# The load of the joint exp-and-ln tables held behind the last eight silus instead of the one traced last

## The chip, the core and the metric

The kernel runs on one core of a Trainium2 chip. The metric is the device time of one execution in microseconds (us), as the median of the runs. Beside the runs there is one profiled execution, whose trace gives the start and the length of each instruction on each engine. PE is the matmul engine, DVE the vector engine, ACT the engine that evaluates functions such as exp, ln and silu from tables, POOL the general-purpose engine, SP the engine that issues most of the DMAs. Every engine works through its own instructions strictly in their order.

## The reference, cut to what matters

The kernel computes a trunk of two layers on an input of 512 tokens by 1024 columns. Layer 0 mixes tokens by attention, layer 1 by a gated delta rule; each mixer stands between two half-step SwiGLU feed-forward networks (FFNs). All is float32, and the matmuls are made of three passes over split operands to keep that precision. The change concerns the first FFN, which uses silu, and the attention that follows it, which uses exp and ln:

```
def swiglu(h, w_gate, w_up, w_down):
    return (jax.nn.silu(h @ w_gate) * (h @ w_up)) @ w_down

# stick-breaking attention, block of 128 queries (4 heads of 128)
z = jnp.einsum('bqhd,bkhd->bhqk', qb, k) * scale
log_beta = jax.nn.log_sigmoid(z)
log_keep = jnp.where(earlier, jax.nn.log_sigmoid(-z), 0.0)
log_after = lax.cumsum(log_keep, axis=3, reverse=True) - log_keep
a = jnp.where(earlier, jnp.exp(log_beta + log_after), 0.0)
return jnp.einsum('bhqk,bkhd->bqhd', a, v)
```

The other four heads use differential attention, which is a softmax (exp, no ln) with a subtraction.

## The kernel before

Activations are kept transposed, as eight tiles of 128 columns by 512 tokens. Weights come in panels of 512 KB by DMA (tile `raw`), which ACT rounds into `wh` (line 173) and DVE turns into the remainder `wl` (line 174); three buffers of each are in rotation. `mm3` (lines 180 to 182) then makes three matmuls of each pair. The matmuls collect in tiles called `mm` (two buffers), `pa` and `pb` (three each).

The first FFN ends in the function `seven`, whose silus are at line 534: four of them, of 128x256, for each pair of hidden tiles. Behind it `even_mixer` opens the attention and calls `exp_ln_tables`, which adds an instruction to ACT's stream that loads the table set holding both exp and ln. [...] A scheduler decides where each instruction stands in its engine's stream, by dependences; the load has no data, so it is tied by hand to an activation that it must stand behind. Once the streams are fixed, the build goes through ACT's stream and adds a load of its own in front of each activation whose function is not in the set then held.

The attention runs in four groups of two heads, two of differential attention (`diff_block`), then two of stick-breaking attention (`sb_block`). While the blocks of one group are worked, the projections of the next group, or the output projection, run between them on PE. In each of the two stick-breaking groups eight blocks (two heads by four query blocks of 128x128 to 128x512) go through this chain, up to three at a time:

```
        nc.vector.tensor_tensor(z[:, :n], ps[:, :n], strict[:, (3 - i) * P:], op=ALU.add)
        nc.scalar.activation(e[:, :n], z[:, :n], AF.Abs)
        nc.scalar.activation(e[:, :n], e[:, :n], AF.Exp, scale=-1.0)
        nc.scalar.activation(e[:, :n], e[:, :n], AF.Ln, bias=1.0)
        nc.vector.scalar_tensor_tensor(s[:, :n], z[:, :n], 0.0, e[:, :n], ALU.max, ALU.add)
        nc.vector.tensor_tensor_scan(r[:, :n][:, ::-1], self.ones.broadcast_to([P, n]),
        nc.vector.tensor_tensor(r[:, :n], z[:, :n], r[:, :n], op=ALU.subtract)
        nc.scalar.activation(r[:, :n], r[:, :n], AF.Exp)
        aT = self.trans_block(pool, r, i)
```

In the profile these are lines 811 (z), 813 (abs), 815 (exp), 816 (ln), 819 (s), 822 (scan), 825 (subtraction) and 826 (the second exp). `trans_block` turns r by PE transposes (line 799) and copies them from `pa` (line 801, on ACT); line 832 multiplies with the values, and line 834 copies the result out. Line 663 scales the projected queries out of an `mm` tile on DVE, line 374 adds the output projection to x on DVE, and line 790 copies a finished differential head out of `pa` on ACT.

Of the kernel before, what the change touches and what calls it, by code (L numbers as in the profile page):

```python
# [12 lines left out]
AF = mybir.ActivationFunctionType  # L13
# [74 lines left out]
class Ordered:  # L88


    def __init__(self, tc):
        self.tc, self.engine = tc, tc.nc.tensor
# [8 lines left out]
class Trunk:  # L101
# [4 lines left out]
    def __init__(self, ctx, tc):  # L106
        self.tc = tc
        self.nc = tc.nc
        self.const = ctx.enter_context(tc.tile_pool(name="const", bufs=1))
        self.xp = ctx.enter_context(tc.tile_pool(name="xp", bufs=1))  # L110
        self.wp = ctx.enter_context(tc.tile_pool(name="wp", bufs=4))
        self.np_ = ctx.enter_context(tc.tile_pool(name="np", bufs=2))
        self.ps = ctx.enter_context(tc.tile_pool(name="ps", bufs=2, space=bass.MemoryType.PSUM))
        self.dram = ctx.enter_context(tc.tile_pool(name="dr", bufs=1, space=bass.MemoryType.DRAM))
        self.ahead, self.pending, self.pin = [], [], None
        self.te = self.nc.tensor
        self.x = [self.xp.tile([P, T], F32, name=f"x{c}") for c in range(KC)]
        self.consts()
# [65 lines left out]
    def exp_ln_tables(self):  # L184

        nc = self.nc
        ld = nc.scalar.add_instruction(mybir.InstLoadActFuncSet(
            name=nc.get_next_instruction_name(), act_func_set_id=EXP_LN_SET, ins=[], outs=[]))
        dep = mybir.DependencyInfo(mybir.DependencyClass.NoSync, mybir.DependencyReason.DATA)
        self.tc.add_manual_dep(ld.ins, self.last_act.ins.name, dep, reason="tables")  # L190
        return ld, dep


# [222 lines left out]
    def eight(self, pool, wg, wu, f, first):  # L416

        nc = self.nc
        g = self.proj_pair(wg, f * P, (self.a_ps, self.b_ps) if f == 2 else None,
                           2 if first and f == 0 else 1)  # L420
        u = self.proj_pair(wu, f * P, (self.a_ps, self.b_ps))
        for j in range(2):
            gr, sg, ur, hd = (self.small(pool, t) for t in ("gr", "sg", "ur", "hd"))
            nc.vector.tensor_tensor(gr, g[j], self.rb, op=ALU.mult)
            self.last_act = nc.scalar.activation(sg, gr, AF.Silu)
            nc.vector.tensor_tensor(ur, u[j], self.rb, op=ALU.mult)
            nc.vector.tensor_tensor(hd, sg, ur, op=ALU.mult)  # L427
            yield hd
# [35 lines left out]
    def seven(self, pool, wg, wu, f):  # L464

        nc = self.nc
        x8 = lambda t: t.rearrange("p (x c) -> p x c", x=8)
        def load(eng, v, kh, lo, hi, **kw):  # L470
            for q, w in enumerate((wg, wu)):
                eng.dma_start(v[:, q * 4:q * 4 + 4], w[kh * 512:(kh + 1) * 512,  # L472
                                                       f * P + lo:f * P + hi]
                              .rearrange("(k p) c -> p k c", p=P), **kw)
        raw = lambda: x8(self.wp.tile([P, 1024], F32, tag="raw", name="raw", bufs=NRAW))
        add = dict(accum_op=ALU.add)
        b11 = x8(pool.tile([P, 1024], F32, tag="sb", name="sb"))
        load(nc.sync, b11, 0, 0, P)
        b2 = x8(pool.tile([P, 2048], F32, tag="sr", name="sr"))
        load(nc.sync, b2, 1, 0, 2 * P)  # L480
        t1, t3 = x8(pool.tile([P, 1024], F32, tag="t1", name="t1")), raw()
        load(nc.sync, t1, 0, 0, P)
        load(nc.gpsimd, t1, 0, P, 2 * P, **add)
        load(nc.sync, t3, 0, P, 2 * P)
        load(nc.gpsimd, t3, 1, P, 2 * P, **add)
        b21, b22 = b2[:, :, :P], b2[:, :, P:]
        X, Y, Z = self.mm_ps(), self.a_ps(), self.b_ps()

        def product(ps, o, right, start=False):
            h = x8(self.wp.tile([P, 1024], F32R, tag="wh", name="wh", bufs=NSPL))  # L490
            l = x8(self.wp.tile([P, 1024], F32R, tag="wl", name="wl", bufs=NSPL))
            self.split_to(h, l, right)
            ah, al = self.left[o]
            for q in range(2):
                out = ps[:, q * 256:(q + 1) * 256]
                for k in range(4):
                    a = [t[k // 2][:, k % 2] for t in (ah, al)]
                    for i, (wt, xt) in enumerate(((h, a[0]), (h, a[1]), (l, a[0]))):
                        nc.tensor.matmul(out, lhsT=wt[:, q * 4 + k], rhs=xt,  # L499
                                         start=start and q + k + i == 0,  # L500
                                         stop=q == 1 and k == 3 and i == 2, skip_group_check=True)

        def combine(tag, a, b, op):
            t = self.small(pool, tag)
            nc.vector.tensor_tensor(t, a, b, op=op)
            return t

        product(X, 0, b11, True)
        p1 = self.np_.tile([P, T], F32, tag="acc", name="p1", bufs=1)
        nc.scalar.copy(out=p1, in_=X)  # L510
        t2 = raw()
        with self.tc.issue_after(self.met) if self.met else nullcontext():
            nc.vector.tensor_tensor(t2, t1, b22, op=ALU.add)
        product(Y, 1, t2, True)
        u2 = self.np_.tile([P, T], F32, tag="sq", name="u2")
        nc.vector.tensor_tensor(u2, p1, Y, op=ALU.add)
        product(Z, 2, t1, True)
        product(Y, 3, t3)
        u3 = self.np_.tile([P, T], F32, tag="sq", name="u3")
        nc.vector.tensor_tensor(u3, p1, Y, op=ALU.add)  # L520
        c22 = self.small(pool, "gr")
        self.met = nc.vector.tensor_tensor(c22, Z, u3, op=ALU.subtract).ins
        product(X, 4, b21)
        t4 = raw()
        nc.vector.tensor_tensor(t4, t2, b21, op=ALU.add)
        product(Y, 5, t4)
        c21 = combine("ur", p1, Y, ALU.add)
        product(Z, 6, b22)
        c12 = combine("ur", Z, u2, ALU.subtract)
        for lo, hi in ((X, c21), (c12, c22)):  # L530
            sg, hd = self.small(pool, "sg"), self.small(pool, "hd")
            for i, c in enumerate((lo, hi)):
                s = slice(i * 256, (i + 1) * 256)
                self.last_act = nc.scalar.activation(sg[:, s], c[:, :256], AF.Silu)
                nc.vector.tensor_tensor(hd[:, s], sg[:, s], c[:, 256:], op=ALU.mult)
            yield hd

# [791 lines left out]
```

## Time and profile before

| | us |
|---|---|
| median of 3 runs | 2018.27 |
| lowest and highest run | 2018.04 and 2020.41 |
| the profiled execution, its own time | 2018.62 |
| its span, first to last instruction | 2016.9 |
| PE busy in the span | 1967.6 (98%) |
| DVE busy | 1304.0 (65%) |
| ACT busy | 897.3 (44%) |

The span begins with the first instruction; 1.7 us of the profiled execution's time lie outside it. Busy shares are means over stages with different limits: one stage can wait for an engine that is idle half of the time in the whole.

### The profile page before, as it was taken

How to read it: one execution, taken by the hardware profiler on the slowest of the kernel's cores; microseconds unless marked ns; L12 is line 12 of the kernel's file. 1: busy time of each engine (PE TensorE's matmuls, PEld its weight loads, DVE VectorE, ACT ScalarE, POOL GpSimd, SP SyncE). 2: the span in 40 equal slices, each digit the busy share in tenths (PEclk: the TensorE clock that was granted, in tenths of full speed). 3: DMA queues.
4: the chain of work that ended last, by engine and by line, in shares of the span. 5: the costliest groups of instructions: out<-in, count | busy, mean ns of one | idle time of the engine just before them, and what ended most of it. 6: DMA issues, size and time to landing. Idle time of an engine off the chain costs nothing.

```text
span 2016.9 us, 29447 instructions
## 1 busy us (share of the span) xinstructions
PE 1967.6 (98%) x11514; PEld 1720.1 (85%) x11514; DVE 1304.0 (65%) x2058; ACT 897.3 (44%) x1577; POOL 254.6 (13%) x394
## 2 busy tenths in 40 slices
PE   8999999999899999999999999998899999999998
PEld 7899898888778899998889999876787788888887
DVE  6867485796557776575677667577577575443543
ACT  5434254466874344353334434455455453222322
POOL 1021110100000021110103011005441400000000
PEclk9999999999999999999999999999999999999999
DMA  7568453221135487543648654344333233322331
GB/s 200 151 132 209 92 128 105 88 83 53 47 88 136 127 171 176 114 105 106 156 131 173 167 125 95 106 116 107 80 81 86 72 110 94 95 94 94 97 101 73
DMA packets 291263, 230.28 MB, mean 114 GB/s; under 512 B 31618, under 2 KB 266420, under 8 KB 291124
## 3 DMA queue, kind: packets, MB, share of 16 engines
q1 hardware_dynamic: 209604, 195.21, 31.7%
q0 software_dynamic: 50688, 25.17, 10.2%
q10 hardware_dynamic: 30832, 8.02, 1.7%
q8 instruction: 90, 1.47, 0.3%
q14 instruction: 49, 0.40, 0.1%
HBM read 223.10 MB, written 5.26 MB: 113 GB/s over the span
## 4 chain that ended last, share of the span: by engine, by line
PE 60%; POOL 5%; DMA 2%; DVE 2%; issue 1%; ACT 1%; ACTq 0%; POOLq 0%; DVEq 0%
PE pa L499 7%; PE pa L182 5%; PE pa L180 5%; PE pa L181 5%; PE pb L182 5%; PE pb L180 5%; PE pb L181 5%; PE mm L95 5%; PE pb L499 5%; PE mm L499 5%; PE mm L181 3%; PE mm L182 3%; PE mm L180 3%; POOL tmp L1162 2%; POOL rr L1165 2%
## 5 line engine op out<-in xcount | busy, mean ns | idle before, releaser
L174 DVE TENSOR_TENSOR wl<-raw,wh 128x1024 fp32r<-128x1024 f32 (+1 forms) x252 | 295.4, 1173 | 271.6 <-ACT wh L173 270.7
L173 ACT CAST wh<-raw 128x1024 fp32r<-128x1024 f32 (+1 forms) x252 | 254.4, 1010 | 427.8 <-PE pb L181 153.5
L180 PE MATMUL mm<-xnh,wh 128*128 128x512 f32 (+1 forms) x432 | 168.7, 394 | 7.9 <-DVE qT L663 5.6
L182 PE MATMUL mm<-xnh,wl 128*128 128x512 f32 (+1 forms) x432 | 168.6, 392 | 0.0
L181 PE MATMUL mm<-xnl,wh 128*128 128x512 f32 (+1 forms) x432 | 168.2, 390 | 0.0
L226 DVE TENSOR_TENSOR wl<-raw,wh 128x1024 fp32r<-128x1024 f32 x72 | 88.0, 1223 | 79.0 <-ACT wh L225 79.0
L225 ACT CAST wh<-raw 128x1024 fp32r<-128x1024 f32 x72 | 75.5, 1049 | 113.6 <-PE pb L499 43.9
L95 PE MATMUL mm<-xnh,wh 128*128 128x512 f32 x256 | 109.1, 426 | 12.9 <-DVE cx L1051 12.9
L499 PE MATMUL pa<-sx,wh 128*128 128x256 f32 x576 | 109.9, 283 | 0.0
L180 PEld LDWEIGHTS mm<-xnh,wh 128*128 128x128 f32 x432 | 82.9, 192 | 25.5 <-DVE qT L663 6.6
L181 PE MATMUL pa<-hid,wh 128*128 128x512 f32 x264 | 102.8, 389 | 0.0
L182 PE MATMUL pa<-hid,wl 128*128 128x512 f32 x264 | 102.7, 389 | 0.0
L181 PE MATMUL pb<-hid,wh 128*128 128x512 f32 x264 | 102.7, 389 | 0.0
L182 PE MATMUL pb<-hid,wl 128*128 128x512 f32 x264 | 102.7, 389 | 0.0
L180 PE MATMUL pa<-hid,wh 128*128 128x512 f32 x264 | 102.3, 389 | 0.0
L180 PE MATMUL pb<-hid,wh 128*128 128x512 f32 x264 | 102.2, 389 | 0.0
L472 POOL DMA_DIRECT2D raw<-in_ffn_w_gate_dram x24 | 30.9, 1289 | 561.0 <-DMA raw<-in_ffn_w_gate_dram 306.8
L95 PE MATMUL mm<-xnl,wh 128*128 128x512 f32 x256 | 101.6, 397 | 0.0
L95 PE MATMUL mm<-xnh,wl 128*128 128x512 f32 x256 | 101.5, 396 | 0.0
L182 PEld LDWEIGHTS mm<-xnh,wl 128*128 128x128 f32 x432 | 82.7, 191 | 15.9 <-issue 0.5
L181 PEld LDWEIGHTS mm<-xnl,wh 128*128 128x128 f32 x432 | 82.8, 192 | 15.6 <-issue 0.2
L225 ACT CAST hid<-hd 128x512 fp32r<-128x512 f32 x88 | 54.5, 619 | 81.3 <-DVE hd L427 72.9
(395 smaller groups left out, 5626.8 us busy)
## 6 DMA issues: line engine op xcount, KB each, us to landing
raw<-in_ffn_w_down_dram SPq DMA_DIRECT2D x88, 512.0 KB, 3.7
raw<-in_ffn_w_gate_dram SPq DMA_DIRECT2D x40, 512.0 KB, 3.7
raw<-in_ffn_w_up_dram SPq DMA_DIRECT2D x40, 512.0 KB, 3.6
raw<-in_gdn_w_in_dram SPq DMA_DIRECT2D x32, 512.0 KB, 3.9
sr<-in_ffn_w_gate_dram SPq DMA_DIRECT2D x24, 512.0 KB, 3.8
sr<-in_ffn_w_up_dram SPq DMA_DIRECT2D x24, 512.0 KB, 4.9
raw<-in_att_w_in_dram SPq DMA_DIRECT2D x24, 512.0 KB, 3.6
sb<-in_ffn_w_gate_dram SPq DMA_DIRECT2D x24, 256.0 KB, 3.8
```

Source lines behind the costliest of these rows:

```text
L95: return self.tc.keep_in_program_order(self.engine.matmul(*args, **kw))
L173: nc.scalar.copy(out=h[:, :n], in_=raw[:, :n])
L174: nc.vector.tensor_tensor(l[:, :n], raw[:, :n], h[:, :n].bitcast(F32), op=ALU.subtract)
L180: self.te.matmul(out, lhsT=lh, rhs=rh, start=start, stop=False)
L181: self.te.matmul(out, lhsT=lh, rhs=rl, start=False, stop=False)
L182: self.te.matmul(out, lhsT=ll, rhs=rh, start=False, stop=stop)
L225: nc.scalar.copy(out=h, in_=src)
L226: nc.vector.tensor_tensor(l, src, h.bitcast(F32), op=ALU.subtract)
L472: eng.dma_start(v[:, q * 4:q * 4 + 4], w[kh * 512:(kh + 1) * 512, f * P + lo:f * P + hi] .rearrange("(k p) c -> p k c", p=P), **kw)
L499: nc.tensor.matmul(out, lhsT=wt[:, q * 4 + k], rhs=xt, start=start and q + k + i == 0, stop=q == 1 and k == 3 and i == 2, skip_group_check ...
L1162: nc.gpsimd.tensor_tensor(p, rr[:, :k, j:j + 1].broadcast_to(sh), lb[:, j, j + 1:].rearrange("p (o m) -> p o m", o=1) .broadcast_to(sh), o ...
L1165: nc.gpsimd.tensor_tensor(rr[:, :k, j + 1:], rr[:, :k, j + 1:], p, op=ALU.subtract)
```

## The change

The silus are gathered in a list, and the hand-made tie of the load is made to each of the last eight instead of to the one that was traced last. The eight are those of the last two pairs of hidden tiles.

```
-        self.ahead, self.pending, self.pin = [], [], None
+        self.ahead, self.pending, self.pin, self.silus = [], [], None, []
...
-        self.tc.add_manual_dep(ld.ins, self.last_act.ins.name, dep, reason="tables")
+        for act in self.silus[-8:]:
+            self.tc.add_manual_dep(ld.ins, act.ins.name, dep, reason="tables")
...
-            self.last_act = nc.scalar.activation(sg, gr, AF.Silu)
+            self.silus.append(nc.scalar.activation(sg, gr, AF.Silu))
...
-                self.last_act = nc.scalar.activation(sg[:, s], c[:, :256], AF.Silu)
+                self.silus.append(nc.scalar.activation(sg[:, s], c[:, :256], AF.Silu))
```

One line more in the function moves the numbers of all later lines up by one in the changed kernel: the silu at line 534 is at line 535 there, the ln of line 816 at line 817.

ACT's stream at the end of the first FFN, before the change. `sg` is the output of a silu, `ur` its input, `hid` a finished hidden tile; the load at line 187 is the one that `exp_ln_tables` adds, and that at line 534 one that the build added.

```order
L534 ACTIVATE sg<-gr 128x256
L187 ACT_TABLE_LOAD
L173 CAST wh<-raw 128x1024
L534 ACT_TABLE_LOAD
L534 ACTIVATE sg<-ur 128x256
L173 CAST wh<-raw 128x1024
L225 CAST hid_3276<-hd 128x512
L534 ACTIVATE sg<-ur 128x256
L225 CAST hid_3285<-hd 128x512
```

The same place in the changed kernel:

```order
L535 ACTIVATE sg<-gr 128x256
L173 CAST wh<-raw 128x1024
L535 ACTIVATE sg<-ur 128x256
L173 CAST wh<-raw 128x1024
L226 CAST hid_3276<-hd 128x512
L535 ACTIVATE sg<-ur 128x256
L187 ACT_TABLE_LOAD
L226 CAST hid_3285<-hd 128x512
```

The load of line 187 has moved behind the last two silus, and the load at line 534, which brought silu's set back, is gone.

ACT's stream in the first stick-breaking group, before the change; `e` and `r` are the tiles of the chain above.

```order
L801 COPY aT<-pa 128x128
L816 ACT_TABLE_LOAD
L816 ACTIVATE e<-e 128x384
L826 ACT_TABLE_LOAD
L826 ACTIVATE r<-r 128x256
L816 ACT_TABLE_LOAD
L816 ACTIVATE e<-e 128x384
L813 ACTIVATE e<-z 128x512
L815 ACT_TABLE_LOAD
L815 ACTIVATE e<-e 128x512
L816 ACT_TABLE_LOAD
L816 ACTIVATE e<-e 128x512
```

The same place in the changed kernel:

```order
L802 COPY aT<-pa 128x128
L817 ACTIVATE e<-e 128x384
L827 ACTIVATE r<-r 128x256
L817 ACTIVATE e<-e 128x384
L814 ACTIVATE e<-z 128x512
L816 ACTIVATE e<-e 128x512
L817 ACTIVATE e<-e 128x512
```

The activations stand in the same order, and every load between them is gone. Over the whole program ACT has 30 loads fewer: 28 in the two stick-breaking groups (16 and 12), the one at line 534, and one at line 626, the first exp of the attention. The streams of PE, DVE, POOL and SP are the same in both kernels, row by row.

## Rows read from the trace of the kernel before

**Rows 1.** Busy us by stretch: window, length, PE, PEld, DVE, ACT, POOL, clock, DMA, GB/s

```profile
312.00:330.00 18.00, 18.00 (x113) 16.22 (x112) 10.74 (x15) 9.47 (x13) 0.00 (x0) 1.00 0.41 133
384.00:394.00 10.00, 10.00 (x75) 9.53 (x75) 9.77 (x18) 9.62 (x14) 0.00 (x0) 1.00 0.18 54
486.00:524.00 38.00, 29.07 (x140) 22.48 (x139) 18.23 (x44) 35.39 (x58) 2.06 (x2) 0.91 0.09 28
548.00:584.00 36.00, 31.51 (x139) 24.34 (x137) 21.97 (x41) 34.78 (x60) 0.00 (x0) 0.91 0.12 37
```

**Rows 2.** PE's waits from 484 to 602: total, times, longest

```profile
PE mm L180 <- DVE qT L663: 5.6, 1, 5.6
PE pa L832 <- ACT aT L801: 4.1, 3, 2.0
PE pa L799 <- ACT r L826: 2.0, 1, 2.0
PE mm L180 <- DVE x L374: 1.4, 1, 1.4
PE pa L799 <- ACT mf L790: 1.0, 1, 1.0
```

**Rows 3.** ACT's groups by line: count, busy us, mean ns, idle before

```profile
L816 ACT ACT_TABLE_LOAD x14 | 18.0, 1283 | 0.2
L826 ACT ACT_TABLE_LOAD x9 | 11.5, 1283 | 0.2
L815 ACT ACT_TABLE_LOAD x5 | 6.4, 1283 | 0.1
...
L816 ACT ACTIVATE e<-e 128x128 f32<-128x128 f32 (+3 forms) x16 | 7.3, 468 | 0.2
...
L534 ACT ACT_TABLE_LOAD x1 | 1.3, 1283 | 0.0
```

**Rows 4.** ACT in order of time, stick-breaking groups: start, length

```profile
490.73 1.28 ACT L816 ACT_TABLE_LOAD   x1
...
513.06 1.28 ACT L816 ACT_TABLE_LOAD   x1
514.36 0.52 ACT L816 ACTIVATE e<-e 128x384 f32<-128x384 f32 x1
...
551.45 1.28 ACT L816 ACT_TABLE_LOAD   x1
...
577.68 1.28 ACT L816 ACT_TABLE_LOAD   x1
```

**Rows 5.** DVE in order of time: start, length, in brackets the wait before

```profile
514.91 0.56 DVE L819 SCALAR_TENSOR_TENSOR s<-z,e 128x384 f32<-128x384 f32 x1 [3.01 <-ACT e L816]
515.39 0.68 DVE L663 SCALAR_TENSOR_TENSOR qT<-mm,rb 128x512 f32<-128x512 f32 x1
```

**Rows 6.** Busy time around PE's low clock, columns as in rows 1

```profile
512.00:516.00 4.00, 0.00 (x0) 0.00 (x0) 1.09 (x2) 3.94 (x6) 0.00 (x0) 0.63 0.00 0
516.00:520.00 4.00, 3.88 (x9) 3.08 (x10) 0.75 (x3) 3.96 (x8) 0.00 (x0) 0.52 0.00 0
568.00:574.00 6.00, 5.18 (x15) 4.37 (x16) 5.30 (x9) 5.91 (x10) 0.00 (x0) 0.50 0.11 32
```

**Rows 7.** PE in order of time, first and last of runs of 128x512 matmuls

```profile
516.12 0.79 PE L180 MATMUL mm<-xnh,wh 128*128 128x512 f32 x1 [5.63 <-DVE qT L663]
...
520.01 0.40 PE L180 MATMUL mm<-xnh,wh 128*128 128x512 f32 x1
...
556.14 0.39 PE L182 MATMUL mm<-xnh,wl 128*128 128x512 f32 x1
...
558.18 0.39 PE L180 MATMUL mm<-xnh,wh 128*128 128x512 f32 x1
```

**Rows 8.** ACT's waits from 484 to 600: total, times, longest

```profile
ACT r L826 <- DVE r L825: 2.2, 4, 0.9
...
ACT e L813 <- DVE z L811: 0.7, 1, 0.7
```

## Prediction

> **What bounds the kernel now.** I read four views, from coarse to fine. The page's busy shares put PE at 98% of the span, so the change can gain only where PE waits or runs slowly. The granted clock in the page's slices is full nearly everywhere; busy time by stretch shows where it isn't. Two stretches stand out, the two stick-breaking groups [rows 1]: from 486 to 524 PE is busy for 29.07 of 38 us and ACT for 35.39, from 548 to 584 PE for 31.51 of 36 and ACT for 34.78, both at a mean clock of 0.91. There ACT is the full engine; DVE is busy about half of the time (18.23 and 21.97). At the end of the first FFN and at the attention's first exp PE is busy for all of 18 and all of 10 us [rows 1].
>
> What PE waits for there is in its waits [rows 2]: 5.6 us for a query projection that DVE has to take out of an `mm` tile, 4.1 for the copies of turned blocks, 2.0 for a block's last exp, 1.4 for DVE's addition to x, and 1.0 for a copy that frees a `pa` tile. Together they are 14.1 us. Three of the five groups name ACT outright. The longest leads to ACT by one step more [rows 5]: DVE's qT at 515.39 stands right behind an s that had waited 3.01 us for ACT's ln, and that ln began at 514.36, just behind a table load [rows 4].
>
> What fills ACT is seen in its groups by line [rows 3]: 14 + 9 + 5 = 28 table loads of 1283 ns, 35.9 us in the two groups. Half of ACT's work in the two stretches (35.39 + 34.78 = 70.2 us) is loads.
>
> [...]
>
> **The change, part by part.**
>
> *The load of line 187* moves from ahead of the last two silus to behind them. It still lasts 1.28 us, and behind it stands only a cast of a hidden tile. Two loads stood ahead of that cast, now one does. PE has no idle time there before (18.00 of 18.00) [rows 1], and nothing comes later than it did: 0.
>
> *The load of line 534* [rows 3] and the one at line 626 of the same length go. PE is fully busy at both places [rows 1], the cover is the projection and output matmuls that run on, and so they give 0.
>
> *The 28 loads of the stick-breaking groups* go. ACT gets 28 x 1.283 = 35.9 us back. How much of it is PE's is the question. The streams of all engines are otherwise the same, row by row, so I ask of each PE wait whether ACT gets there early enough without the loads that stand ahead of it. For the qT wait, 11 of the 16 loads of the first group stand ahead, the first at 490.73 and the last at 513.06 [rows 4]: 11 x 1.283 = 14.1 us. For PE never to wait there, qT must come earlier by the wait itself, 5.6, and by what PE gained before it (2.0 + 1.0): 8.6 us. So 5.5 us are to spare. ACT will use some of that up: with its loads gone it will itself wait for DVE's scans and subtractions. Before, such waits were 2.2 us in four times over both groups [rows 8], because ACT was the late one. Following the two streams from row to row with their present durations I get qT at about 505 us against a need at 507.5 (516.12 less 8.6, [rows 7]), an estimate with some 2 us to spare.
>
> In the second group the last wait is the one for x. Of its 12 loads 11 stand ahead, from 551.45 to 577.68 [rows 4]: again 14.1 us freed. Needed are at most that wait of 1.4, all of the aT waits, 4.1, and 2.6 of clock (below): 8.1 us. At least 6.0 are to spare, of which the row-by-row estimate leaves some 3. So I take all five groups of waits as gone: **14.1 us**. The bounds are 0, if DVE's part of the chain holds everything up, and 14.1.
>
> *The clock.* What the low clock cost is PE's busy time at it times the share withheld [rows 6]: 3.88 x 0.48 = 1.9 and 5.18 x 0.50 = 2.6, together **4.5 us**. A second row agrees: nine matmuls took from 516.12 to 520.01, 3.89 us, and nine of the same shape at full clock from 556.14 to 558.18, 2.04 us [rows 7], a loss of 1.85. The clock fell only behind waits, so without them I take it as full. The bounds are 0 and 4.5.
>
> [...]
>
> *The sum* is 14.1 + 4.5 = 18.6 us. The profiled execution took 2018.62 (span 2016.9 and 1.7 around it), so 2000.0. The median of the runs shown is 0.35 us lower, 2018.27, and I predict it less 18.6: **1999.7 us**.
>
> **The rivals.**
>
> *Part of it comes back as waits for DVE.* Between a block's ln and its second exp stand three DVE steps (s, scan, subtraction), DVE works in order, and qT stands behind two s. If the hops cost more than my rows give them, the qT wait stays. For it: the estimate leaves only some 2 us. Against it: DVE is half idle in both stretches, and 14.1 us are freed for 8.6 needed. It decides once ACT's new waits for DVE ahead of qT pass 5.5 us. If the whole qT wait with its clock stayed, 5.6 + 1.9 = 7.5 of the gain would go: 2007.2; a small remnant of 2 or 3 us gives 2002 to 2003.
>
> *The change doesn't do what it says, or the loads were hidden.* If what PE waited for is set by DVE alone, the time stays at 2018.3. Against it: the loads are gone from the built stream, and the ln that DVE waited for stood directly behind one. For it only that ACT is 44% busy overall, a mean over stages.
>
> *Slower: the joint set is slower for each activation.* No exp or ln of the stick-breaking blocks ran under the joint set before, so no row has its price. Exp and ln have three groups like the one of line 816, 7.3 us each [rows 3], 22 us in both stick-breaking stretches. For ACT to have as much work as before they would have to take (22 + 35.9)/22 = 2.6 times as long. At three times, ACT would have 22 x 2 - 35.9 = 8 us more to do than before, PE would wait for it, and the time would be about 2026.4. Nothing in the trace speaks for it. [...] No run here shows the joint set for these lines yet.
>
> **How the numbers follow.** My forecast, with remnants of waits up to 3 us, has 0.83. A larger remnant, the qT wait above all, has 0.12; no gain 0.03; the slower set 0.02. More than 18.6 can come only from gaps too short to be listed, some 1 to 2 us. The range goes down by these and by the spread of a median, to 1997.3, and up to 2005, between the small remnants and the full qT wait, which leaves under 2 in 10 outside. A change of 0.2%, 4 us, is about what a measurement of this kernel can tell from none. The forecast and the larger remnant are both faster by more: 0.95 less a little for a remnant near the whole, 0.94. Within it lies the case without gain and that little, 0.04; slower 0.02.
>
> **What would show each step.** In the changed kernel's profile: no table load between the attention's first exp and the next FFN's first silu; ACT well below full in the two groups, near 20 us of work each, with more waits for DVE's r and z; PE's waits for qT, aT, r, x and mf gone or under 0.5 us each; clock 1.0 throughout both groups; exp and ln at 468 ns as before; everything behind the attention unchanged but earlier by some 18 us. I am wrong on the size if a qT or aT wait of several microseconds is still there with DVE, not ACT, as the late engine, or if the clock still falls. I am wrong on the mechanism if the waits go and the same time turns up again later, for instance as waits for weights in the FFN behind the attention.

## The result

The changed kernel takes 1998.47 us (median of 4 runs, 1997.62 to 1999.38) against 2018.79 us (4 runs), a ratio of 0.9898 with a 95% interval of 0.9881 to 0.9916: 20.3 us faster, forecast 18.6. A second series gave 1997.5 against 2019.34, a ratio of 0.9892 (0.9876 to 0.9909). The profiled executions are 19.24 us apart, 2018.62 and 1999.38 (span 1997.6).

In the rows below, lines above 190 are higher by one than in the rows of before. The first view is busy time by stretch, columns as in [rows 1]. The two stretches of the first FFN's end and the attention's first exp come first; then the two stick-breaking groups, which now lie at 486 to 513 and 536 to 567; the last row is both groups with what lies between and behind them.

```profile
312.00:330.00 18.00, 18.00 (x116) 16.38 (x115) 11.42 (x15) 8.90 (x12) 0.00 (x0) 1.00 0.37 119
384.00:394.00 10.00, 10.00 (x72) 9.41 (x71) 9.74 (x20) 7.69 (x13) 0.00 (x0) 1.00 0.17 54
486.00:513.00 27.00, 27.00 (x148) 22.36 (x147) 20.45 (x47) 20.15 (x50) 2.11 (x2) 1.00 0.16 49
536.00:567.00 31.00, 31.00 (x155) 25.22 (x154) 23.99 (x43) 21.72 (x54) 0.00 (x0) 1.00 0.16 52
...
486.00:582.00 96.00, 96.00 (x547) 81.99 (x546) 62.43 (x113) 57.45 (x133) 4.60 (x4) 1.00 0.23 70
```

PE is busy for all of 96 us and the clock is full. ACT, nearly full before, has 20.15 of 27 and 21.72 of 31. PE's view of waits has no row at all between 480 and 590. What has taken the place of its waits is seen on ACT, whose longest waits over 480 to 590 are these (total, times, longest), to be set against [rows 8]:

```profile
ACT wh L173 <- PE mm L181: 11.6, 6, 4.3
ACT r L827 <- DVE r L826: 6.7, 9, 2.1
ACT mf L835 <- PE pa L833: 6.1, 6, 2.4
ACT e L814 <- DVE z L812: 3.4, 4, 1.3
```

The waits for `r` and `z` were 2.2 and 0.7 us before [rows 8]. The other two were there before too, with 7.1 and 3.5 us from 484 to 600. So ACT now waits more for PE and DVE, and PE no longer waits for it. Exp and ln are no slower under the joint set (ACT's groups by line, 480 to 590; 468 ns was the mean before [rows 3]):

```profile
L827 ACT ACTIVATE r<-r 128x128 f32<-128x128 f32 (+3 forms) x16 | 7.5, 471 | 6.8 <-DVE r L826 6.7
L817 ACT ACTIVATE e<-e 128x128 f32<-128x128 f32 (+3 forms) x16 | 7.3, 466 | 0.2
L816 ACT ACTIVATE e<-e 128x128 f32<-128x128 f32 (+3 forms) x16 | 7.3, 466 | 0.2
```

The place of the longest wait, in order of time on DVE and then on PE (start, length, wait before), answers to [rows 5] and [rows 7]:

```profile
503.39 0.56 DVE L820 SCALAR_TENSOR_TENSOR s<-z,e 128x384 f32<-128x384 f32 x1 [0.16 <-ACT e L817]
504.22 0.69 DVE L664 SCALAR_TENSOR_TENSOR qT<-mm,rb 128x512 f32<-128x512 f32 x1 [0.27 <-PE mm L182]
```

```profile
507.11 0.40 PE L182 MATMUL mm<-xnh,wl 128*128 128x512 f32 x1
507.35 0.40 PE L180 MATMUL mm<-xnh,wh 128*128 128x512 f32 x1
```

qT is done at 504.91, and PE comes to need it at 507.35: 2.4 us to spare, where the prediction had estimated 505, 507.5 and some 2. The s ahead of it waits 0.16 us for the ln instead of 3.01, and qT itself now waits for PE.

Where the time went can be followed by pairing each matmul with itself, since PE's stream is the same in both kernels. The offset of the changed kernel (its start less that of before) moves like this:

```
matmul (line before)           before    changed   offset
L182 at the attention's start  379.68    380.55    +0.87
L799, waited for r             501.22    499.90    -1.32
L799, waited for mf            507.98    505.39    -2.59
L180, waited for qT            516.12    507.35    -8.77
L180, clock full again         520.01    509.43   -10.58
L832, waited for aT            530.80    518.80   -12.00
L832, waited for aT            565.88    551.87   -14.01
L832, waited for aT            568.82    552.57   -16.25
L181, clock full again         574.51    555.51   -19.00
L180, waited for x             584.42    563.59   -20.83
```

The +0.87 arose at the start: 0.28 of it because the input's transfers landed later, the rest at 14.8 to 15.4 of the kernel before, where its matmuls already follow each other by 0.12 us and those of the changed kernel still by 0.21. From +0.87 to -20.83 the changed kernel gains 21.7 us in the two groups, 13.0 in the first (up to -12.11) and 8.7 in the second. Behind them the offset is flat up to the gated delta rule. Past it the profiled run is left with 1.6 us less, which makes the 19.24 of the two profiles. This is not a price of the change: in the profile of the changed kernel run again (below) less than 0.3 us is lost there, and the gain in the groups is the same to 0.01 us.

### The profile page after: what moved, and what is told of

It is laid out like the page before. It is cut to its first block, busy times and chain, and to the rows that moved or that the text cites. A ratio compares the mean times of both kernels' runs of the same rounds, so it can differ in the third digit from the quotient of the medians.

```text
span 1997.6 us, 29417 instructions
## 1 busy us (share of the span) xinstructions
PE 1964.2 (98%) x11514; PEld 1720.2 (86%) x11514; DVE 1304.8 (65%) x2058; ACT 859.6 (43%) x1547; POOL 255.2 (13%) x394
## 4 chain that ended last, share of the span: by engine, by line
PE 88%; POOL 5%; DVE 2%; DMA 2%; issue 1%; ACT 1%; ACTq 0%; SPq 0%; POOLq 0%; DVEq 0%
PE pa L500 10%; PE pb L500 7%; PE mm L500 7%; PE pa L182 6%; PE pa L180 6%; PE pa L181 6%; PE pb L182 6%; PE pb L180 6%; PE pb L181 6%; PE mm L180 6%; PE mm L181 6%; PE mm L182 6%; PE mm L95 4%; POOL tmp L1163 2%; POOL rr L1166 2%
## 5 line engine op out<-in xcount | busy, mean ns | idle before, releaser
L500 PEld LDWEIGHTS pa<-sx,wh 128*128 128x128 f32 x576 | 89.9, 192 | 0.0
```

Source lines behind the costliest of these rows:

```text
L500: nc.tensor.matmul(out, lhsT=wt[:, q * 4 + k], rhs=xt, start=start and q + k + i == 0, stop=q == 1 and k == 3 and i == 2, skip_group_check ...
```

## The experiments

Each run keeps the streams of PE, DVE, POOL and SP as they are and changes only which loads stand in ACT's stream. So its matmuls can be paired like those above. What a run loses in the two groups against the profile of the changed kernel is given "by pairing" beside the times: the change of the offset from 484 to 530 us and from 530 to 600 us of the changed kernel. Loads put in for an experiment have no line of their own in the profile; they show as idle time of some 1.3 us ahead of the activation, by "issue".

**The 28 loads back, under the joint set.** After the streams are fixed, a load of the joint set is put ahead of each marked exp or ln at which the kernel before changed sets:

```
+            for k, ins in enumerate(seq):
+                mark = MARKS.get(ins.name)
+                if mark:
+                    kind, grp, i = mark
+                    need = "ln" if kind == "ln" else "exp"
+                    if need != held and True:
+                        at.append(k)
+                    held = need
+            for k in reversed(at):
+                block.instructions.insert(k, mybir.InstLoadActFuncSet(
...
```

> The changed kernel with 28 loads of the joint set put back at the places in the two stick-breaking groups where the kernel before had loads; exp and ln still run under the joint set and nothing else differs. Theory (ACT's time in the 28 loads holds PE there): the time of before, 2018.8 us, within 2, with PE's waits for qT, aT, r, x and mf back at about 14 us and the granted clock back at about 0.91 in both groups. Rival (what cost time was the change of sets, or exp and ln under their separate sets, not the loads as such): the time of the changed kernel, 1998.5.

Measured: 2019.55 us against 2018.76, a ratio of 1.0004 (0.9995 to 1.0014). PE's waits from 480 to 602 and, below, busy time in the two stretches:

```profile
PE mm L183 <- DVE qT L667: 6.0, 2, 5.6
PE pa L836 <- ACT aT L805: 4.1, 3, 2.0
PE pa L803 <- ACT r L830: 2.2, 2, 2.0
PE mm L183 <- DVE x L378: 1.5, 1, 1.5
```

```profile
486.00:524.00 38.00, 29.93 (x141) 23.21 (x140) 18.14 (x44) 17.31 (x44) 2.06 (x2) 0.91 0.10 28
548.00:584.00 36.00, 31.40 (x140) 24.25 (x138) 21.98 (x41) 19.39 (x48) 0.00 (x0) 0.91 0.12 37
```

Waits, low clock and time are back, with exp and ln under one set. By pairing, this run loses 21.7 us in the groups, 13.0 and 8.7, just what the change had gained. It is the time that the loads take on ACT, at these places, and nothing else of the sets.

One thing expected did not come back: PE's wait for `mf` has no row. Instead the clock fell already behind the wait for `r`:

```profile
504.00:508.00 4.00, 4.00 (x13) 2.56 (x13) 2.23 (x4) 2.73 (x6) 0.00 (x0) 0.79 0.00 0
```

The group's loss is 13.0 us all the same. So how the loss divides into waits and low clock can differ between executions, while its sum stays: PE, slowed behind `r`, came later to the place where it had waited for `mf`.

**One load, elsewhere.** The kernel before with its tie and its two loads at the FFN's end untouched, and one load of the joint set ahead of the attention's first exp:

```
                 ex = nc.scalar.activation(le, ls, AF.Exp)
+                MARKS[ex.ins.name] = True
...
+                mark = MARKS.get(ins.name)
+                if mark:
+                    at.append(k)
```

> The kernel before, its two loads at the end of the first FFN kept as they are, with one load of the joint set ahead of the attention's first exp in place of the build's; the 28 loads of the stick-breaking groups fall away by that. Theory (the loads outside the two groups are hidden): the time of the changed kernel, 1998.5 within 1.5. Rival (the loads at the end of the first FFN and at the first exp cost PE their length too): 1.3 to 2.6 us more than the changed kernel, 1999.8 to 2001.1.

Measured: 1997.49 us (1997.1 to 1998.89), a ratio of 0.9898 (0.9881 to 0.9914), and PE without a row of waits in the groups, where by pairing it loses 0.00 us against the changed kernel. The whole gain comes from the joint set being held when the groups begin; the tie as such and the loads outside are worth nothing that can be measured.

**No load by hand.** The kernel before with the load of line 187 taken out of the finished stream, with which the one at line 534 goes too:

```
+                if isinstance(block.instructions[k], mybir.InstLoadActFuncSet):
+                    del block.instructions[k]
```

> The kernel before without its load made by hand, so that silu's set stays at the end of the first FFN; two loads fewer there, the 28 in the stick-breaking groups as before. Theory: the time of before, 2018.8 within 1.5, since these two are hidden and the load by hand did nothing where it stood. Rival (these two cost PE their length): 2016.2.

Measured: 2019.11 us against 2018.76, a ratio of 1.0002 (0.9993 to 1.0011); by pairing the groups lose 21.7 us, as in the kernel before. Two loads fewer at a covered place are worth nothing, and the load made by hand had no effect where it stood: silu's set came back behind it, and the build fell into loading exp's and ln's own sets by turns.

**One load ahead of each ln.** The condition of the first run becomes `if kind == "ln":`, 16 loads.

> The changed kernel with one load of the joint set ahead of each of the 16 ln of the stick-breaking blocks, 16 x 1.283 = 20.5 us of ACT's time. Theory (PE waits only where ACT's delay passes what is to spare, which in the changed kernel's trace is 2.4 us at qT, and ACT had idle time of its own): 6 loads, 7.7 us, stand ahead of the first qT, of which 2 to 5 come through; both groups together lose 2 to 10 us, 2001 to 2008.5, my value 2004. Rival (each load costs PE the same share): 16/28 of the 20.3 us, 11.6, so 2010.

Measured: 2010.95 us (2008.84 to 2011.63), a ratio of 0.996 (0.9946 to 0.9975). My value was too low by 7 us, the time lies above my 2001 to 2008.5, and the rival's 2010 was met. PE's waits in this run (480 to 602):

```profile
PE mm L183 <- DVE qT L667: 3.6, 1, 3.6
PE mm L183 <- DVE x L378: 3.5, 3, 1.6
PE pa L836 <- ACT aT L805: 1.7, 1, 1.7
```

The wait for qT, 3.6 us, is within the 2 to 5 that I gave it. I had named neither the waits for x and aT in the second group, 5.2 us, nor the clock, which fell again behind the long wait, as busy time by stretch shows:

```profile
511.00:517.00 6.00, 5.87 (x16) 4.77 (x17) 4.04 (x8) 3.23 (x8) 0.00 (x0) 0.54 0.01 3
```

5.87 x 0.46 = 2.7 us of low clock and 8.8 of waits make 11.5 of the 12.5 that were lost against the changed kernel (by pairing 12.9, 6.3 and 6.6 in the two groups).

**Eight loads.** As the run before, with `if kind == "ln" and i in (0, 3):`: the smallest and the largest blocks.

> The changed kernel with 8 loads of the joint set, one ahead of the ln of each smallest (128x128) and each largest (128x512) stick-breaking block; 10.3 us of ACT's time. Threshold theory (PE waits only for what passes the time to spare, 2.4 us at the first qT, some 3 at the second qT and at x, plus idle time that ACT itself has): two loads stand ahead of the first qT, three of the second, at most four of x, so at most about 3 us are lost over both groups, 1998.5 to 2001.5. Rival (each load costs PE the same, 20.3/28 = 0.73 us): 5.8 us, 2004.3. The run with 16 loads agreed with the rival's number; this one tells them apart.

Measured: 1999.29 us (1998.47 to 2002.03), a ratio of 0.9905 (0.989 to 0.9919), 0.8 to 1.8 us over the two series of the changed kernel, with intervals that overlap; by pairing the groups lose 2.7 us. The threshold theory's 2001.5 holds, and the rival's 2004.3 is out. PE's waits are 1.6 and 0.3 us, and the clock stays full in the groups:

```profile
PE mm L183 <- DVE x L378: 1.6, 2, 1.3
PE pa L836 <- ACT aT L805: 0.3, 1, 0.3
```

So loads don't cost the same each. By pairing, half as many as in the run before cost a fifth, 2.7 of 12.9 us. That fits the theory that up to a point they fall into ACT's own idle time and what is to spare, and that past it the waits come in full and bring the low clock with them; ACT's idle time was not followed load by load. That 16 loads met the proportional number was chance.

**One group at a time.** The rule of the first run with `grp == 0` (16 loads) and with `grp == 1` (12 loads).

> The changed kernel with the 16 loads of the first stick-breaking group put back at their places, none in the second. Theory: the two groups lose independently, and matmul by matmul the first group gained 13.0 us of 21.7: 1998.5 + 13.0 = 2011.5, within 2. Rival (the second group's waits follow from the first group's lateness): the whole, 2018.8.

> The changed kernel with the 12 loads of the second stick-breaking group put back, none in the first. Theory: 1998.5 + 8.7 = 2007.2, within 2. Rival (the second group's waits follow from the first group's lateness): 1998.5.

Measured: 2011.19 us (ratio 0.9962, 0.9948 to 0.9976) and 2006.89 us (0.994, 0.9925 to 0.9955). The groups lose independently, 12.7 and 8.4 us over 1998.47, by pairing 13.0 and 8.8, each with 0.00 in the other group. PE's waits in the run with the second group's loads alone (480 to 602), where the qT wait of the first is missing:

```profile
PE pa L836 <- ACT aT L805: 3.5, 2, 2.0
PE mm L183 <- DVE x L378: 1.4, 1, 1.4
PE pa L803 <- ACT r L830: 0.7, 1, 0.7
```

**The same in the gated delta rule.** Its set-up has one exp and one ln in turn, each behind a load of its own in the changed kernel; one load of the joint set ahead of the exp replaces both.

```
+        MARKS[nc.scalar.activation(e, e, AF.Exp, scale=-1.0).ins.name] = True
...
+                mark = MARKS.get(ins.name)
+                if mark:
+                    at.append(k)
```

> The changed kernel with the joint set loaded once ahead of the exp and ln that set up the gated delta rule, where the build has a load ahead of each; one load more falls away there, and another moves behind to a later tanh. Theory (the ln's load holds the only wait of PE for this chain, 0.7 us in the changed kernel): that wait goes, 0.7 to 0.9 us, 1997.7, less than the runs can tell. Rival (the load that moves to the later tanh delays the convolutions, for which PE waits 11 us): the same time or up to 1.3 us more.

> The changed kernel again, as the measure for the next run on the same chip. Theory: 1998.5 within 1, and no wait of PE of over 0.5 us in the two stick-breaking groups.

> The kernel of the run e8_gdn_joint again, beside the changed kernel. If the 1.7 us between their medians is the saved load, it is 0.7 to 1.7 us below the run e9_changed_again here too, with intervals that hardly overlap; if it is the spread from run to run, the two agree within 0.5.

Measured: 1996.73 us (0.989, 0.9875 to 0.9904), then 1997.5 for the changed kernel again and 1996.73 (0.9887, 0.9872 to 0.9902) for this one beside it. PE's waits over the whole of the changed kernel have a row, for a tile of that set-up, that is missing in both runs of this one:

```profile
PE pa L95 <- DVE gyy L974: 0.7, 1, 0.7
```

That wait is gone, and the difference of 0.8 us beside each other has the size expected, but the intervals overlap widely: the profile shows the saved wait, the runs can't confirm the time. The run of the changed kernel had no row of PE's waits in the two groups, as expected.

## Why the prediction was right

*What bounded the kernel* was read rightly: PE in the whole, ACT in the two groups. The first run shows ACT's loads as the cause, and the runs by group show where. One count was loose: two of the 28 loads begin behind 524, at 525.21 and 527.58, so 26 of them, 33.4 us, make up just under half of ACT's 70.2 us in the two stretches.

*The loads at lines 187, 534 and 626* were put at 0. The runs with one load and without a load by hand show it.

*The waits* were put at 14.1 us, all gone. They are all gone, but were worth more: the offsets jump at the seven waits by 2.19, 1.19, 5.79, 0.78, 1.75, 2.14 and 1.69, together 15.5. At each the profile shows 0.1 to 0.3 us less as idle time than the next matmul was really late, because the end that the profile gives a matmul lies behind the time at which the next could have begun: the 128x512 matmuls are given 0.39 us each, and nine of them follow one another in 2.04 us [rows 7], 0.23 apart.

*The clock* was put at 4.5 us. From 516.12 to 520.01 the offset moves by 1.81 and from 568.82 to 574.51 by 2.75, together 4.6. Here the measurement agrees with PE's busy time at the low clock alone; the stretch from 512 to 516, in which PE did nothing at a mean clock of 0.63 [rows 6], is in the waits. That waits and clock could be added is true of the execution shown; the first run divides the same loss in another way.

*The rest* of the 21.7, 1.6 us, lies in gaps of 0.1 to 0.4 us that no list of waits shows; the prediction allowed 1 to 2 for them. The sum was thus 3 us too small in the groups, and 1.6 of it were lost again later in the profiled run. That the first medians came out only 1.7 us beyond the forecast is thus in part luck: those of the second series are 21.8 us apart, the groups' whole gain, and its 1997.5 lies barely within the 1997.3 to 2005 that was forecast.

*To spare at qT* were 2.4 us, as estimated. The rival of DVE taking over did not come about. ACT's waits for it have grown to 10.1 us in both groups (6.7 + 3.4 above, for `r` and `z`), from 2.9. Ahead of qT, from 484 to 504, they are 2.3 us, where the rival needed 5.5; before, there were none:

```profile
ACT e L814 <- DVE z L812: 1.8, 2, 1.3
...
ACT r L827 <- DVE r L826: 0.5, 2, 0.2
```

*The slower set* is out by 466 ns against 468 and by the first run. *No gain* is out by the result.

*What a load took on ACT* is its 1283 ns [rows 3] and next to nothing around it: the load at 513.06 begins 0.01 us after the exp ahead of it has ended (512.63, 0.42 long), and the ln at 514.36 begins 1.30 us after the load [rows 4]. ACT's own waits in the first run give the same for a load put in, 18.4/14 = 1.31:

```profile
ACT e L820 <- issue: 18.4, 14, 1.3
```

## What to carry to other kernels

Look at which table set ACT holds at each place of the built stream, and not only at where the load was asked for: a load tied to one activation can be undone by another that the scheduler puts behind it, without any error. Judge loads by the stage: 28 of them took 1.8% of the span, in a stage where ACT set the pace, and cost more than half of their length, while three elsewhere cost nothing that could be measured. And PE's stalls cost more here than their idle time: 14.1 us of listed waits stood for 21.7, through the clock and the gaps around. Where two kernels have the same streams, pairing each matmul with itself tells more than the medians: it gave the loss in the groups alike to 0.1 us in every profile with the same loads, while single runs of one kernel lie up to 3.6 us apart (the kernel before, 2016.75 to 2020.39).

## What the runs showed that was not expected

The clock falls for some waits and not for others of nearly the same length. In the gated delta rule PE waits for a tile `kdec`, 2.97 us in the profiled run of before and 3.26 us in that of the changed kernel. Behind it the first kept its clock, the second didn't (busy time by stretch, before and then changed):

```profile
1353.00:1358.00 5.00, 4.16 (x31) 3.90 (x31) 5.00 (x15) 2.54 (x9) 0.00 (x0) 1.00 0.41 110
```

```profile
1333.00:1338.00 5.00, 4.66 (x21) 4.09 (x22) 5.00 (x14) 2.04 (x7) 0.00 (x0) 0.66 0.51 144
```

The offset moves from -20.8 to -18.9 there, 0.3 of it by the longer wait. The length of the wait alone doesn't decide: in the second run of the joint set in the gated delta rule the wait was shorter than either, 2.73 us, and the clock behind it fell as well:

```profile
1332.00:1337.00 5.00, 5.00 (x26) 4.49 (x26) 5.00 (x11) 1.84 (x6) 0.00 (x0) 0.66 0.65 188
```

What does decide stays open. Nor is it the reason that the two profiled runs of the changed kernel differ by 2.2 us: the faster, 1997.18, waited 3.22 us for `kdec`, and its clock fell behind that wait too (0.53 from 1331 to 1338).
